# Attention of a hybrid block: values in two bursts, the query's norm in the exponential, and another spread of the filling work

## The chip, the cores and the metric

The kernel runs on one core of one Trainium2 chip. The metric is the device time of one launch in microseconds (us), as the median of several runs. A profile is one further execution, recorded by the hardware profiler; its rows give starts and durations of single instructions on the engines: PE (TensorE matmul) with PEld (its weight loads), DVE (VectorE), ACT (ScalarE), POOL (GpSimd) and SP (which here only issues DMAs).

## What is computed

The reference is a model of two layers over 512 latent tokens and 256 context tokens of width 1024: layer 0 mixes the tokens by attention, layer 1 by a state-space scan, and a gated feed-forward network follows each. The change touches only the attention, cut here to what matters:

```
q_l = rms_norm(q_l.reshape(bsz, seq, N_HEADS, HEAD_DIM), q_norm)    # 16 heads of 64
k_l = rms_norm(k_l.reshape(bsz, seq, N_KV_HEADS, HEAD_DIM), k_norm) # 4 key heads
q_l = apply_rope(q_l, cos, sin);  k_l = apply_rope(k_l, cos, sin)   # latent tokens only
s = jnp.einsum('bqhgd,bkhd->bhgqk', q, k) * (HEAD_DIM ** -0.5)
p = jax.nn.softmax(s, axis=-1)
o = jnp.einsum('bhgqk,bkhd->bqhgd', p, v)
x = x + mod_l[2] * (o.reshape(bsz, seq, Q_DIM) @ w_o)
```

Latent queries see all 768 keys; context queries see the 256 context keys. The norm of a query is one number per token and head: it multiplies the query's whole row of scores, so it can be applied before the scores are formed or after.

## The kernel before, in words

Activations lie transposed, with channels on the 128 partitions and tokens along the free axis. Products that need full precision are done by `mm3` (line 100): operands are split in a rounded high part and a low part in the type fp32r, and three matmuls add high·high, high·low and low·high. The attention's `score` (line 589) keeps both parts of a query stacked on the partitions, so two matmuls do. Transposes of probabilities (line 626) and the products with the values (line 638) are plain fp32; PE runs each value product as two passes.

**Units.** The 16 heads are handled in 8 pairs, p = 0 to 7. A pair has three units: `hf` 0 and 1 are 256 latent queries each against 768 keys, `hf` 2 the 256 context queries against 256 keys. Unit n = 3p + hf; there are 24. `a_steps` (line 597) makes a unit's scores and softmax: four score tiles of 128 queries by 768 keys, or four of 128 by 256 in two PSUM tiles. `softmax` (line 570) is a row maximum on DVE, the exponential with its sum on ACT, then a reciprocal and a scaling on DVE. `b_steps` (line 616) is the other half: for each of 6 (or 2) key tiles four transposes into one PSUM bank, a copy to SBUF (two of three on ACT, one on DVE, line 630), and, one step later, the product with the values for that key tile into the bank `ps_o`. The output is copied to `g.o[p]` (line 640).

**The loop** (lines 677 to 703) runs unit n's `a_steps` beside unit n-1's `b_steps`, a step of each in turn, and after every step `fill.run(us)`.

**Fill.** `Fill` (line 176) is a queue of generators with other work. `run(us)` takes pieces in order until their stated costs are over the budget `us`; a piece that returns `BREAK` costs 1.0 and rests for 5 calls. `require` runs a generator to its end at once. In the queue are the norm and rotation of keys and queries (`keys`, `queries`), the projection of the queries of pairs 4 to 7 (first half of `queries`, line 547), eight pieces `ada` (line 111, gains and biases from the conditioning: 2 MB of weights each), and, from pair 7 on, `project` (line 1221): the output projection w_o for pairs 0 to 2 and 3 to 4, through `down` (line 708), which adds the product to the residual `X` by one DVE instruction a tile (line 726). The last part of w_o, pairs 5 to 7, comes after the loop (line 1240). The budget is 0.65 us a step, 1.3 from unit 21 on.

**A query's preparation** (`normed`, line 512): square on ACT (`qsq`), gain on ACT, a swap of rows by four DMAs, three instructions of rotation (on POOL for most pairs), then `rstd_rows` (line 227): matmuls with a block of ones give sums over the 64 channels (`ssq`, line 236), some DVE and ACT instructions of 12 columns give the reciprocal root, one DVE instruction spreads it to 768 columns (`rbq`, line 247), six PE transposes turn it (`rsTq`, line 253), and two DVE instructions multiply the query (line 526). Then the casts to high and low parts (lines 564, 565).

**Order of the work.** In the first part of the attention (lines 392 to 489) the order is written out by hand. Behind it a planner orders the instructions of each engine: it takes them by program order as soon as, by its own model of durations, their inputs and tile slots are there; a later instruction can go ahead of one that has to wait. Each engine then executes that list strictly in order. What limits it are slots: 27 tiles `t3` of 768 columns, 6 tiles `t2` of 512, 10 tiles `t4` for weights, and in PSUM two tiles `S` for scores (two banks each) and four banks `B` for everything else.

Of the kernel before, what the change touches and what calls it, by code (L numbers as in the profile page):

```python
# [7 lines left out]
P = 128  # L8
# [102 lines left out]
def ada(g, src, layer, chunks, m0, nm, big=True):  # L111
# [17 lines left out]
    sb = g.t3p.tile([P, 512], F32, tag="t2", bufs=6, name="ada_sb")  # L129
# [41 lines left out]


# [54 lines left out]
def rstd_rows(g, sq, n, cols, width, name, bank):  # L227
# [16 lines left out]
    nc.vector.scalar_tensor_tensor(u, y, -0.5, u, ALU.mult, ALU.mult)  # L244
    rb = t3(g, f"rb{name}", n=n)
# [133 lines left out]
def attention(g, fill, X, late):  # L379
# [5 lines left out]
    t2 = lambda name, dt=F32: g.t3p.tile([P, 512], dt, tag="t2", bufs=6, name=name)  # L385
# [126 lines left out]
    def normed(qs, gain, eng):  # L512
# [9 lines left out]
        eng.tensor_tensor(qs[:, :L], qs[:, :L], sw, ALU.add)  # L522
        for r in rstd_rows(g, sq, T, g.blk, HD, "q", Bk):
            if r is not BREAK:
                pt, c0, c1 = r
                nc.vector.tensor_tensor(qs[:, c0:c1], qs[:, c0:c1], pt[:, : c1 - c0], ALU.mult)
            yield BREAK

    k2 = {}

    def keys(j, qs, eng):
        yield from normed(qs, kn, eng)
# [11 lines left out]
    qprep = {}  # L544

    def queries(p, qs, eng):
        if qs is None:
            w = load_w(g, I["wq"][p - 4], lo_engine="pool")
            qs = t3(g, "qs")
            for h, c0, n in ((hc, L, C), (hl, 0, L)):  # L550
                ps = Bk("ps_q")
                for k in range(KT):
                    ks = slice(k * P, (k + 1) * P)
                    mm3(g, (w[0][:, ks], w[1][:, ks]), [(ps[:, :n], h[k])], k == 0, k == KT - 1)
                    yield 3 * n / 2400
                nc.scalar.copy(qs[:, c0 : c0 + n], ps[:, :n])
            yield BREAK
        yield from normed(qs, g.qn8, eng)
# [11 lines left out]
    def softmax(pr, ps):  # L570
        mx = g.p.tile([P, 1], F32, tag="mx", bufs=4, name="mx")
        nc.vector.reduce_max(mx, ps, axis=AX.X, negate=True)
        sm = g.p.tile([P, 1], F32, tag="sm", bufs=4, name="sm")
        nc.scalar.activation(pr, ps, AF.Exp, bias=mx, accum_out=sm)
# [5 lines left out]
    class Unit:  # L580
# [16 lines left out]
        def a_steps(self):  # L597
            for e in range(2):
                if self.hf < 2:
                    for t in range(2):  # L600
# [3 lines left out]
                        softmax(pr, ps[:, :T])  # L604
                        self.pr[e, t] = pr
                        yield
                else:
                    ps, pr = Sb("ps_sc"), t2("prc")
                    for t in range(2):
# [3 lines left out]
                        softmax(self.pr[e, t], o)  # L613
                    yield

        def b_steps(self):

            nkt = self.nk // P
            po = None
            pts = []  # L620
            for kt in range(nkt + 1):
                if kt < nkt:
                    ps = Bk("ps_pt")
                    for e in range(2):
                        for t in range(2):
                            nc.tensor.transpose(ps[:, e * 256 + t * P : e * 256 + (t + 1) * P],  # L626
                                                self.pr[e, t][:, kt * P : (kt + 1) * P], g.ident)
                    pT = t2("pT")
                    copies[0] += 1
                    (nc.vector.tensor_copy if copies[0] % 3 == 0 else nc.scalar.copy)(pT, ps)  # L630
                    pts.append(pT)
                yield
                if kt:
                    if po is None:
                        po = Bk("ps_o")
                    v = vt[self.k0 // P + kt - 1][:, self.kv * HD : (self.kv + 1) * HD]
                    for e in range(2):
                        nc.tensor.matmul(po[S64[e], :256], v, pts[kt - 1][:, e * 256 : (e + 1) * 256],  # L638
                                         start=kt == 1, stop=kt == nkt)
# [733 lines left out]
```

## Time and profile before

| what | value |
|---|---|
| median of 3 runs (lowest, highest) | 1967.96 us (1965.83, 1969.62) |
| the profiled execution | 1956.99 us, its span 1955.2 us |
| PE, DVE, ACT, POOL busy in the span | 98%, 69%, 45%, 15% |
| attention loop and output projection in the trace (first score to last `ps_d` row before the tail) | 94.6 to about 443.4 us |
| of that, pairs 0 to 3 | 94.6 to 264.8 us |
| pairs 4 to 7, up to the last unit's first score | 264.8 to 391.5 us |
| the rest of the units and of w_o | 391.5 to 443.4 us |

How to read it: a row of the timeline has start, duration, engine, line, operation, output and inputs, shape and a count of merged instructions; a bracket at its end gives the idle time before it and what ended it. Matmuls are pipelined, so that the duration of one is longer than the time from its start to the start of the next; the time that PE spends on something is read from starts. Busy shares of PE are therefore no measure of how well it is used.

### The profile page before, as it was taken

Reading aid. Unit: us, or ns where it says so; the run is one execution under the profiler, and the core shown is the slowest. Engines: PE = TensorE matmul, PEld = TensorE weight load, DVE = VectorE, ACT = ScalarE, POOL = GpSimd, SP = SyncE. Lnnn points to the kernel's source line nnn. Section 1 sums busy time; section 2 is a strip of 40 time slices with the busy share of each in tenths; the row PEclk is TensorE's granted clock in tenths of the full one; section 3 lists DMA queues with packets and bytes.
Section 4 is the critical chain, followed back from the end, with each engine's and each line's share of the span. In section 5 each row is a group of like instructions: output and inputs, shape, how many; then the busy total and the mean of one; then the engine's idle time right before and its main releaser. Section 6 shows DMA issues by size and latency. Waiting matters only on the chain.

```text
span 1955.2 us, 28359 instructions
## 1 busy us (share of the span) xinstructions
PE 1909.6 (98%) x11068; PEld 1595.4 (82%) x11068; DVE 1346.6 (69%) x2119; ACT 885.1 (45%) x1636; POOL 297.5 (15%) x272
## 2 busy tenths in 40 slices
PE   8999999998999999999999999999999999999999
PEld 6866776688888888888888888888888888888887
DVE  4557778667877777775568777778878566555555
ACT  3645676436222222222256767666667343333331
POOL 2212201003000000000031233422335210000000
PEclk8999999999999999999999999999999999999999
DMA  8254010012434333332222433433354323333332
GB/s 330 87 183 162 28 33 17 1 55 98 143 125 123 128 124 123 123 106 65 76 87 66 134 119 108 121 116 92 103 162 119 101 74 96 97 97 97 97 98 87
DMA packets 71702, 205.36 MB, mean 105 GB/s; under 512 B 8720, under 2 KB 14224, under 8 KB 71440
## 3 DMA queue, kind: packets, MB, share of 16 engines
q1 hardware_dynamic: 71568, 203.54, 32.5%
q8 instruction: 87, 1.43, 0.3%
q14 instruction: 47, 0.39, 0.1%
HBM read 196.43 MB, written 4.46 MB: 103 GB/s over the span
## 4 chain that ended last, share of the span: by engine, by line
PE 70%; DVE 12%; issue 8%; POOL 4%; ACT 1%; DMA 1%; SPq 0%; POOLq 0%; DVEq 0%; ACTq 0%
PE ps_up L106 10%; PE ps_up L108 10%; PE ps_up L105 10%; PE ps_d L105 6%; PE ps_d L108 6%; PE ps_d L106 6%; PE ps_o L638 3%; PE ps_pt L626 3%; PE ps_s L594 2%; DVE xf L900 2%; POOL E L999 1%; DVE ht L281 1%; PE ps_in L108 1%; DVE E L1009 1%; DVE Bf L900 1%
## 5 line engine op out<-in xcount | busy, mean ns | idle before, releaser
L87 DVE TENSOR_TENSOR wl<-wst,wh 128x1024 fp32r<-128x1024 f32 x205 | 253.1, 1234 | 276.1 <-PE ps_up L106 124.1
L85 ACT CAST wh<-wst 128x1024 fp32r<-128x1024 f32 x211 | 221.1, 1049 | 413.3 <-DMA wst<-in_wup 323.7
L106 PE MATMUL ps_up<-hlf,wh 128*128 128x512 f32 x1008 | 357.0, 354 | 0.0
L105 PE MATMUL ps_up<-hhf,wh 128*128 128x512 f32 x1008 | 356.9, 354 | 0.0
L108 PE MATMUL ps_up<-hhf,wl 128*128 128x512 f32 x1008 | 356.8, 354 | 0.0
L106 PEld LDWEIGHTS ps_up<-hlf,wh 128*128 128x128 f32 x1008 | 190.6, 189 | 26.1
L105 PEld LDWEIGHTS ps_up<-hhf,wh 128*128 128x128 f32 x1008 | 190.5, 189 | 26.2
L108 PEld LDWEIGHTS ps_up<-hhf,wl 128*128 128x128 f32 x1008 | 190.5, 189 | 26.0
L105 PE MATMUL ps_in<-hhs,wh 128*128 128x512 f32 (+1 forms) x560 | 205.0, 366 | 0.0
L108 PE MATMUL ps_in<-hhs,wl 128*128 128x512 f32 (+1 forms) x560 | 199.7, 357 | 0.0
L106 PE MATMUL ps_in<-hls,wh 128*128 128x512 f32 (+1 forms) x560 | 199.5, 356 | 0.0
L105 PE MATMUL ps_d<-hdh,wh 128*128 128x512 f32 (+1 forms) x568 | 193.8, 343 | 1.4 <-DVE X L726 1.2
L108 PE MATMUL ps_d<-hdh,wl 128*128 128x512 f32 (+1 forms) x568 | 193.5, 341 | 0.0
L106 PE MATMUL ps_d<-hdl,wh 128*128 128x512 f32 (+1 forms) x568 | 193.0, 340 | 0.3 <-DVE hdl L87 0.3
L726 DVE SCALAR_TENSOR_TENSOR X<-ps_d,mod,X 128x512 f32<-128x512 f32 (+1 forms) x240 | 133.0, 584 | 31.3 <-PE ps_d L108 30.6
L106 PEld LDWEIGHTS ps_d<-hdl,wh 128*128 128x128 f32 x568 | 106.7, 188 | 15.5 <-DVE hdl L87 0.7
L105 PEld LDWEIGHTS ps_d<-hdh,wh 128*128 128x128 f32 x568 | 106.3, 188 | 15.3 <-DVE X L726 1.6
L105 PEld LDWEIGHTS ps_in<-hhs,wh 128*128 128x128 f32 x560 | 106.3, 190 | 15.1 <-issue 0.9
L108 PEld LDWEIGHTS ps_in<-hhs,wl 128*128 128x128 f32 x560 | 106.2, 190 | 14.9
L108 PEld LDWEIGHTS ps_d<-hdh,wl 128*128 128x128 f32 x568 | 106.7, 188 | 13.3
L106 PEld LDWEIGHTS ps_in<-hls,wh 128*128 128x128 f32 x560 | 106.3, 190 | 13.6
L167 DVE SCALAR_TENSOR_TENSOR junk<-wada,cb 128x1024 f32<-128x1024 f32 x96 | 116.7, 1215 | 1.1 <-ACT cb L159 0.9
(325 smaller groups left out, 3699.7 us busy)
## 6 DMA issues: line engine op xcount, KB each, us to landing
wst<-in_wup SPq DMA_DIRECT2D x88, 512.0 KB, 3.5
wada<-in_adaT SPq DMA_DIRECT2D x48, 512.0 KB, 3.5
wst<-in_win SPq DMA_DIRECT2D x48, 512.0 KB, 3.5
wst<-in_wdown SPq DMA_DIRECT2D x44, 512.0 KB, 4.1
wada<-in_adaB SPq DMA_DIRECT2D x32, 512.0 KB, 7.4
E<-ad SPq DMA_DIRECT2D x64, 256.0 KB, 6.5
ec<-ead SPq DMA_DIRECT2D x64, 128.0 KB, 4.3
wst<-in_wout SPq DMA_DIRECT2D x16, 512.0 KB, 3.5
```

The source lines that it names most:

```text
L85: keep(nc.scalar.copy(hi, src))
L87: keep(eng.tensor_tensor(lo, src, _r(hi), ALU.subtract))
L105: mm(out, wh, ah, start=first, stop=False)
L106: mm(out, wh, al, start=False, stop=False)
L108: mm(out, wl, ah, start=False, stop=last)
L167: g.tc.keep_in_program_order(nc.vector.scalar_tensor_tensor(junk, w, 1.0, cb[:, v * D : (v + 1) * D], ALU.mult, ALU.mult, accum_out=md[:, ...
L281: nc.vector.scalar_tensor_tensor(t[:, c0:c1], ap, g.moda[layer][ca][:, m, v : v + 1], rs[:, c0:c1], ALU.mult, ALU.mult)
L594: nc.tensor.matmul(ps[:, c0 : c0 + n], qprep[self.p][e][:, q0 : q0 + P], kk[:, self.k0 + c0 : self.k0 + c0 + n], start=i == 0, stop=i == 1)
L626: nc.tensor.transpose(ps[:, e * 256 + t * P : e * 256 + (t + 1) * P], self.pr[e, t][:, kt * P : (kt + 1) * P], g.ident)
L638: nc.tensor.matmul(po[S64[e], :256], v, pts[kt - 1][:, e * 256 : (e + 1) * 256], start=kt == 1, stop=kt == nkt)
L726: nc.vector.scalar_tensor_tensor(ap, o[:, c0:c1], gate[:, m, v : v + 1], ap, ALU.mult, ALU.add)
L900: nc.vector.scalar_tensor_tensor(cv, raw[:, tap : tap + n], par(f"sw{tap}", j), cv, ALU.mult, ALU.add)
```

## The change

The change does five things.

1. **Values in two bursts.** `b_steps` no longer multiplies with the values at every key tile. With six key tiles it multiplies three of them behind the fourth tile's transposes and three at the end; with two, both at the end. Within a burst the newest tile comes first.
2. **The norm in the exponential's scale.** `queries` ends its norm with the 12 columns of `rstd_cols` (the first part of the old `rstd_rows`) in a tile `qrs`; no spreading, no transposes, no multiplication of the query. `softmax` multiplies the negated maximum by the norm (a new DVE instruction of one column) and gives the norm to the exponential as `scale`. Keys are normed as before.
3. **Scores every second step.** `a_steps` yields twice after each score tile, so a unit takes 8 steps (before: 4, where both halves were short, else 8): 24 steps a pair instead of 20.
4. **Another queue.** The projections of pairs 4 to 7 are generators of their own, placed in the first half and required before unit 12; six of the eight `ada` are moved from the first half to the second. w_o for pairs 0 to 2 enters the queue at pair 4 and for pairs 3 to 4 at pair 6, and the outputs are split pair by pair.
5. **Budgets and slots.** `PACE` gives 0.5, 0.45, 0.35 us a step by `hf` in the first twelve units, 0.6, 0.5, 0.4 in the next twelve, and 1.0 at the end. `t2` has 8 slots instead of 6, `t3` 26 instead of 27.

```diff
+PACE = ((0.5, 0.45, 0.35), (0.6, 0.5, 0.4), (1.0, 1.0, 1.0))
...
-def rstd_rows(g, sq, n, cols, width, name, bank):
+def rstd_cols(g, sq, n, cols, width, name, bank):
...
     nc.vector.scalar_tensor_tensor(u, y, -0.5, u, ALU.mult, ALU.mult)
+    return u, y
+
+def rstd_rows(g, sq, n, cols, width, name, bank):
+    nc = g.nc
+    c = cols.shape[-1]
+    nt = n // P
+    u, y = rstd_cols(g, sq, n, cols, width, name, bank)
     rb = t3(g, f"rb{name}", n=n)
...
-    t2 = lambda name, dt=F32: g.t3p.tile([P, 512], dt, tag="t2", bufs=6, name=name)
+    t2 = lambda name, dt=F32: g.t3p.tile([P, 512], dt, tag="t2", bufs=8, name=name)
...
+    def projection(p):
+        w = load_w(g, I["wq"][p - 4], lo_engine="pool")
+        yield 0
+        qs = qraw[p] = t3(g, "qs")
...
+    def queries(p, eng):
+        qs = qraw[p]
+        sq = roped(qs, g.qn8, eng)
+        u, y = rstd_cols(g, sq, T, g.blk, HD, "q", Bk)
+        nc.vector.scalar_tensor_tensor(qrs[p], u, 1.5, y, ALU.add, ALU.mult)
+        yield BREAK
         out = []
...
-    def softmax(pr, ps):
+    def softmax(pr, ps, rs):
         mx = g.p.tile([P, 1], F32, tag="mx", bufs=4, name="mx")
         nc.vector.reduce_max(mx, ps, axis=AX.X, negate=True)
+        nc.vector.tensor_tensor(mx, mx, rs, ALU.mult)
         sm = g.p.tile([P, 1], F32, tag="sm", bufs=4, name="sm")
-        nc.scalar.activation(pr, ps, AF.Exp, bias=mx, accum_out=sm)
+        nc.scalar.activation(pr, ps, AF.Exp, bias=mx, scale=rs, accum_out=sm)
...
                         self.pr[e, t] = pr
                         yield
+                        yield
...
         def b_steps(self):
             nkt = self.nk // P
-            po = None
+            half = (nkt + 1) // 2
+            po = Bk("ps_o")
             pts = []
+            def multiply(k0, k1):
+                for kt in reversed(range(k0, k1)):
+                    v = vt[self.k0 // P + kt][:, self.kv * HD : (self.kv + 1) * HD]
+                    for e in range(2):
+                        nc.tensor.matmul(po[S64[e], :256], v, pts[kt][:, e * 256 : (e + 1) * 256],
+                                         start=kt == half - 1, stop=kt == half if nkt > half else kt == 0)
...
+                pts.append(pT)
+                if nkt > 2 and kt == half:
+                    multiply(0, half)
                 yield
...
+            yield
+            if nkt > 2:
+                multiply(half, nkt)
+            else:
+                half = nkt
+                multiply(0, nkt)
             nc.scalar.copy(g.o[self.p][:, self.q0 : self.q0 + 256], po[:, :256])
...
-    fill.q = [vals] + [kgen if o == "k" else adas.pop(0) if o == "a" else qgen[int(o)] for o in "a1aa2aa3aaa4k567"]
+    fill.q = [work[o]() for o in "aPa2Qk3RS4"]
...
             if A.p == 4:
                 fill.require(kgen)
-            if A.p == 7:
-                for p in range(6):
-                    osplit(p)
-                late()
+                for p in range(4, 8):
+                    fill.require(proj[p])
+                fill.q += [work[o]() for o in "5"]
+            if A.p >= 4:
+                while len(g.oT) < A.p - 1:
+                    osplit(len(g.oT))
+                late(A.p)
+                fill.q += [work[o]() for o in {4: "a", 5: "6", 6: "7aa", 7: "aaa"}[A.p]]
...
-            fill.run((.65, 1.3)[0] if n < 21 else (.65, 1.3)[1])
+            fill.run(PACE[n // 12][n % 3])
...
-    g.t3p, g.n3 = pool("pa", pha), 27
+    g.t3p, g.n3 = pool("pa", pha), 26
...
-    def late():
-        for fs in ((0, 1, 2), (3, 4), (5, 6, 7))[:-1]:
+    def late(p):
+        for fs in {4: ((0, 1, 2),), 6: ((3, 4),)}.get(p, ()):
             fill.add(project(fs))
```

In the queue's string a digit is a pair's `queries`, a letter P to S the projection of pairs 4 to 7, `k` the second keys and `a` the next `ada`.

More of the change, by code (lines that the diff above doesn't have):

```diff
@@ L659, in attention @@
             next(vals)
-    qgen = {p: queries(p, raw[{1: 2, 2: 4, 3: 5}[p]] if p < 4 else None, nc.gpsimd) for p in range(1, 8)}
+    qgen = {p: queries(p, nc.gpsimd) for p in range(1, 8)}
+    proj = {p: projection(p) for p in range(4, 8)}
     kgen = keys(1, raw[3], nc.gpsimd)
@@ L680, in attention @@
         if n == 1:
[L681 removed]
             for i, _ in enumerate(vals):
                 if i % 8 == 8 - 1:
[L684 to L685 removed]
+                    next(qgen[1], None)
         if A and A.hf == 0:
```

78 lines of the change are left out of this document (32 added, 46 removed).

## The prediction

> **What bounds the kernel now.** I read the page first, then busy times by stretch, then who waits for whom on PE, then PE's instructions in order of time.
>
> ```profile
> span 1955.2 us, 28359 instructions
> PE 1909.6 (98%) x11068; PEld 1595.4 (82%) x11068; DVE 1346.6 (69%) x2119; ACT 885.1 (45%) x1636; POOL 297.5 (15%) x272
> ```
> ```profile
> 94.60:443.41 348.81, 341.39 (x2234) 243.96 (x2235) 245.47 (x485) 191.07 (x403) 50.88 (x37) 0.99 0.20 67
> 264.80:391.50 126.70, 122.53 (x745) 84.93 (x744) 99.11 (x192) 77.25 (x166) 11.70 (x9) 1.00 0.05 13
> 324.30:354.10 29.80, 26.53 (x161) 16.21 (x160) 25.09 (x51) 18.34 (x40) 4.64 (x3) 1.00 0.03 7
> ```
> ```profile
> PE ps_s L594 <- ACT pr L574: 1.7, 3, 0.8
> ...
> PE ps_pt L626 <- DVE pr L576: 1.1, 2, 0.7
> ...
> PE rsTf L253 <- DVE rbf L247: 0.2, 1, 0.2
> ```
>
> The columns of a stretch are its length, then busy us of PE, PEld, DVE, ACT and POOL with instruction counts, clock, DMA share, GB/s. The attention and its output projection take 348.8 us, with PE busy for 341 of them and DVE for 245. The second fence is the list of PE's waits in that stretch: nine lines, from 1.7 down to 0.2 us, 8.1 us together. So PE is the bound there, almost without named waits; what the change can win must be PE time. The clock is full (0.99), so no gain comes from there.
>
> But busy does not mean that PE streams. The order of time shows it, around one value product between matmuls of w_o:
>
> ```profile
> 389.20 0.39 PE L106 MATMUL ps_d<-hlol,wh 128*128 128x512 f32 x1
> 389.43 0.40 PE L108 MATMUL ps_d<-hhol,wl 128*128 128x512 f32 x1
> 389.75 0.65 PE L638 MATMUL ps_o<-pT,v 128*64 128x256 f32 x4
> 390.33 0.39 PE L105 MATMUL ps_d<-hhoc,wh 128*128 128x256 f32 x1
> 390.56 0.28 PE L106 MATMUL ps_d<-hloc,wh 128*128 128x256 f32 x1
> 390.68 0.28 PE L108 MATMUL ps_d<-hhoc,wl 128*128 128x256 f32 x1
> ```
> ```profile
> 283.99 1.08 PE L638 MATMUL ps_o<-pT,v 128*64 128x256 f32 x8
> 285.00 0.38 PE L594 MATMUL ps_sc<-kh,q 128*128 128x256 f32 x1
> ...
> 285.35 0.60 PE L626 MATMUL ps_pt<-cst,pr 128*128 128x128 f32 x4
> 285.70 0.36 PE L105 MATMUL ps_q<-hha,wh 128*128 128x256 f32 x1
> 285.90 0.28 PE L106 MATMUL ps_q<-hla,wh 128*128 128x256 f32 x1
> ```
> ```profile
> 288.32 0.65 PE L638 MATMUL ps_o<-pT,v 128*64 128x256 f32 x4
> 288.90 0.66 PE L626 MATMUL ps_pt<-cst,pr 128*128 128x128 f32 x4
> 289.31 0.36 PE L105 MATMUL ps_q<-hha,wh 128*128 128x256 f32 x1
> 289.51 0.28 PE L106 MATMUL ps_q<-hla,wh 128*128 128x256 f32 x1
> ```
>
> From start to start a matmul of 512 columns takes 0.23 us in a row of its kind, one of 256 columns 0.12. The one before the value product takes 0.32: 0.09 more. The four passes of one key tile take 0.58 us, but eight take 1.01: the second four cost 0.43, so 0.15 of the 0.58 is paid once per group. The first matmul after it takes 0.23 where 0.12 is usual: 0.11. One **group** of value products costs 0.09 + 0.15 + 0.11 = 0.35 us beyond its work. In front of transposes it is somewhat less: the transposes behind it take 0.41 us (288.90 to 289.31) where they take 0.35 alone, so 0.09 + 0.15 + 0.06 = 0.30. I take 0.32.
>
> **The change part by part.**
>
> *Values in two bursts.* A unit with six key tiles has six groups now and two afterwards; one with two key tiles has two and then one. 16 × 6 + 8 × 2 = 112 groups become 16 × 2 + 8 = 40. The passes stay. 72 × 0.32 = **23.0 us less** on PE. The added waits: a burst needs the newest copy of `pT` first, and behind it on PE's list stand scores and fill; but the other tiles of a burst were copied a step or more earlier. One of the four `B` banks is now held from a unit's beginning; ACT and DVE empty the other banks in 0.6 to 0.7 us, so I charge nothing; if that cover failed, a transpose would wait for about one such copy.
>
> *The norm in the exponential.* On PE it takes away six transposes a query:
>
> ```profile
> L253 PE MATMUL rsTq<-cst,rbq x60: 270/272/332, 79.4 to 334.7; 128*128 128x128 f32 x60
> ```
>
> 60 less the keys' 12 are 48. Four cost 0.35 us alone and 0.41 behind values, 0.09 to 0.10 each: **4.2 us less** (about half, where they join a group of `ps_pt`; at most 4.9). On DVE:
>
> ```profile
> L247 DVE SCALAR_TENSOR_TENSOR rbq<-rsu,rsy 128x768 f32<-128x768 f32 x8 | 9.8, 1224 | 0.2
> L244 DVE SCALAR_TENSOR_TENSOR rsu<-rsy,rsu 128x12 f32<-128x12 f32 x8 | 4.7, 586 | 0.1
> L526 DVE TENSOR_TENSOR raw<-raw,rsTq 128x512 f32<-128x512 f32 x4 | 2.7, 685 | 5.8 <-issue 3.3 <-POOL raw L522 2.5
> L526 DVE TENSOR_TENSOR raw<-raw,rsTq 128x256 f32<-128x256 f32 x4 | 1.7, 413 | 3.0 <-PE rsTq L253 3.0
> ```
> ```profile
> L575 DVE RECIPROCAL sm<-sm x96: 143/155/167, 97.6 to 398.9; 128x1 f32<-128x1 f32 x96
> ```
> ```profile
> L243 DVE TENSOR_TENSOR rsu<-rsy,rsa x21: 149/171/1958, 13.1 to 1589.8; 128x12 f32<-128x12 f32 x10, 128x2 f32<-128x2 f32 x9, 128x4 f32<-128x4 f32 x2
> ```
>
> Eight queries lose about 8 × (1.22 + 0.69 + 0.41) = 18.6 us and get 8 × 0.59 = 4.7 for `qrs`. The 96 new one-column products are not in the trace; by the reciprocal of one column they cost 96 × 0.155 = 14.9 us, by the slowest small product seen 96 × 1.96 = 188, which only the worst instant allows; I take the reciprocal's price. DVE's sum stays about as it is (+1 us), and PE bears nothing. The page "GPSIMD Engine Reference" of the Trainium skill, section Specifications, speaks against this exchange: it says that VectorE contends with GpSimd where an instruction has two SBUF inputs, as the new product has and the reciprocal has not. The rows above agree, with 1958 ns at most against 167; by that rule, with POOL busy for 50.9 of 348.8 us, some 14 of the 96 would be held by up to 1.8 us, an estimate of at most 25 us of DVE time, which would enter the sum only where DVE is the bound.
>
> *Scores every second step, queue, budgets.* The work is the same; its places move. The four projections' weight loads with their POOL splits come earlier, six `ada` with 2 MB each and their DVE copies later, five w_o loads earlier than their place at pair 7. SP has room: the DMA share is 0.05 between 264.8 and 391.5. Pair 6 now has no fill: in the 29.8 us of the third stretch PE is idle for 3.3. With w_o there I take **3 us less**. The other way, the end loses its cover:
>
> ```profile
> 418.11 0.65 PE L638 MATMUL ps_o<-pT,v 128*64 128x256 f32 x4
> ...
> 418.81 0.37 ACT L640 COPY o<-ps_o 128x256 f32<-128x256 f32 x1 [1.65 <-PE ps_o L638]
> ...
> 421.06 0.41 DVE L87 TENSOR_TENSOR hloc<-o,hhoc 128x256 fp32r<-128x256 f32 x1
> ```
>
> The last values are copied and split while PE still does w_o for pairs 3 and 4; from 418.11 to the split's end at 421.47 are 3.4 us. Afterwards only w_o for pairs 5 to 7 is left, which needs this very output: I charge **3 us**. DVE stands at 99.1 of 126.7 us in the second half; with the PE time saved there (half of 27 us) that is 99.1 of 113, or 88%, in stretches without w_o. W_o itself dilutes it: its 120 pairs of products take 120 × (0.23 + 0.12) = 42 us of PE and these DVE instructions:
>
> ```profile
> L726 DVE SCALAR_TENSOR_TENSOR X<-ps_d,mod,X 128x256 f32<-128x256 f32 x29 | 13.9, 482 | 9.4 <-PE ps_d L108 9.3
> L726 DVE SCALAR_TENSOR_TENSOR X<-ps_d,mod,X 128x512 f32<-128x512 f32 x16 | 12.0, 749 | 12.4 <-PE ps_d L108 12.3
> ```
>
> 16 × (0.48 + 0.75) = 19.7 us, 47% of them. For queueing at a fuller DVE I charge **4 us**, an estimate between nothing and the 13.5 us of that half. One `t3` slot less and the four query tiles kept longer cost nothing as long as fill is ready.
>
> **Sum:** -23.0 - 4.2 - 3 + 3 + 4 = -23.2 us. The profiled execution (1956.99 us, 1.8 outside its span) would become 1933.8. The median of the runs shown, 11 us above it, becomes **1944.8 us** (-1.2%).
>
> **The rivals.**
>
> *DVE becomes the bound of the second half.* For it speaks 88%, against it the dilution. The half then keeps its length and its 13.5 us are lost, in place of my 4: -23.2 + 9.5 = -13.7, and with the same in the fuller stretches of the first half -8: 1954 to 1960 us.
>
> *The planner breaks the bursts.* It orders PE's list by its own model and may put ready instructions between. Against it: a burst begins with its newest tile, so all that follows is ready. If all 112 groups remained, only the transposes and the fill count: -4.2 - 3 + 3 + 4, about 0: 1968 us.
>
> *The transposes wait for the softmax (slower).* With six key tiles a unit's last score now comes two steps before the next unit's first transposes; before, it came one step ahead of them in a pair's first unit, but five in its second. The chain, in the stretch without fill:
>
> ```profile
> 338.42 0.50 PE L594 MATMUL ps_s<-kh,q 128*128 128x512 f32 x1 [0.77 <-ACT pr L574]
> 339.42 0.96 DVE L572 TENSOR_REDUCE mx<-ps_s 128x1 f32<-128x768 f32 x1
> 340.41 0.90 ACT L574 ACTIVATE pr<-ps_s,mx 128x768 f32<-128x768 f32 x1 [0.86 <-DVE mx L572]
> 342.41 0.61 DVE L576 TENSOR_SCALAR pr<-pr,sm 128x768 f32<-128x768 f32 x1
> 343.33 0.66 PE L626 MATMUL ps_pt<-cst,pr 128*128 128x128 f32 x4
> ```
>
> That is 4.9 us, and 5.1 with the new product; two steps of 24 a pair are 2 × 300 / 192 = 3.1 us (300 us: the stage afterwards without its tail). Without cover each of the 16 changes behind such a unit costs 2.0 us: +32 - 23 = +9, 1977 us. It decides from 1.45 us a change on. Against it speaks that a pair's first unit has a step less already, and that the waits of `ps_pt` on `pr` sum to 1.1 us in the whole stage.
>
> **How the numbers follow.** Chances: forecast 0.60 (1932 to 1954: waits gone at one end, DVE at the other), more (banks and waits all well) 0.06, DVE bound 0.14, bursts broken or gains cancelled 0.05, slower 0.15. A measurement can tell about 0.2%, 4 us, from no change. Faster 0.60 + 0.06 + 0.14 = 0.80, same 0.05, slower 0.15. The range leaves out the slower rival and the ends of the others: 1930 to 1963.
>
> **What would show it.** Stretches of twelve value passes in PE's order, about 40 in all, each some 0.15 us over 0.107 a pass; no `rsTq` beyond 12; the stretch from the first score to the last w_o product of about 326 us; PE's waits still near 8 us; DVE below 85% in the second half. I am wrong if waits on `pr`, `pT` or `ps_d` of tens of us appear, or if groups number far over 40.

## The result and the profile after

The changed kernel is **slower**: 1974.53 us median of 20 runs (1966.92 to 1981.88) against 1967.68 us (1959.40 to 1976.31) for the kernel before on the same chips, a ratio of 1.0032 with an interval of 1.0018 to 1.0046, or about 6.3 us. The forecast was 1944.8 us, and its range ended at 1963.

The profiled executions stand further apart, 1978.52 us against 1956.99: before's is faster than all its timed runs, after's lies near the upper end of its own. The clock that TensorE is granted differs between them as well: 0.994 and 0.984 as means of the two profiled spans, where the timed runs of the kernel before average 0.9897 (the 111 beside the experiments below) and the 20 of the changed kernel 0.9856. The traces therefore say where time went, and the timed ratios say how much.

The page of the changed kernel, its span, its busy row and its row of granted clock:

```profile
span 1976.7 us, 28337 instructions
...
PE 1903.2 (96%) x11020; PEld 1606.9 (81%) x11020; DVE 1347.1 (68%) x2199; ACT 891.5 (45%) x1636; POOL 298.4 (15%) x272
...
PEclk8998989989999999999999999999999999999999
```

The same row of the kernel before:

```profile
PEclk8999999999999999999999999999999999999999
```

PE is busy for 6 us less, and the span is longer all the same. The clock row has an 8 in slices 4, 6 and 9, all in the attention stage; before has 9 from the second slice on.

Busy times by stretch, from the first score to the first product of the feed-forward input, of the kernel before and then of the changed one (columns: stretch, length, then busy us of PE, PEld, DVE, ACT and POOL, clock, DMA share, GB/s):

```profile
94.00:449.43 355.43, 347.41 (x2286) 249.98 (x2286) 252.06 (x498) 195.91 (x414) 54.10 (x40) 0.99 0.20 66
```
```profile
94.00:465.76 371.76, 343.69 (x2258) 264.87 (x2258) 253.89 (x580) 205.61 (x418) 51.61 (x40) 0.94 0.19 64
```

PE idled for 355.43 - 347.41 = 8.0 us before and idles for 28.1 us now. And the clock is 0.94 where it was 0.99: over these lengths that is 0.06 × 371.76 = 22.3 us of lost clock against 3.6 (an upper bound, since the mean counts idle time too). Without that, PE's busy time is 343.8 us before and 321.4 now: 22.4 us less, where the forecast took away 23.0 + 4.2 = 27.2. So most of the gain is there, and two losses that the forecast did not have are larger: +20.1 us of idling and up to +18.7 of clock, in a stage that is 16.3 us longer.

The clock's part is that large in this pair of executions only. In the timed runs the mean clock falls from 0.9897 to 0.9856, about 8 us of a launch; with the work and the idling of the traces, -22.4 + 20.1 + 8 is +5.7 us, against the 6.3 measured.

The waits of PE in this stage of the changed kernel (us in all, times, longest):

```profile
PE ps_s L618 <- ACT pr L598: 6.6, 7, 2.4
PE ps_sc L618 <- ACT prc L598: 5.4, 6, 1.4
PE ps_s L618 <- DVE q L587: 4.7, 2, 2.8
PE ps_s L618 <- ACT prc L598: 2.5, 3, 1.4
...
PE ps_pt L662 <- DVE pr L600: 1.3, 2, 0.7
```

Three of these rows are a score that waits until an exponential gives back one of the two score tiles, 14.5 us together; one is a score that waits for a query. The waits of the transposes on the softmax, the place of the forecast's slower rival, are 1.3 us.

PE's order of time shows how a short wait becomes a slow stretch:

```profile
152.12 0.28 PE L618 MATMUL ps_s<-kl,q 128*128 128x256 f32 x1
...
154.00 0.50 PE L618 MATMUL ps_s<-kh,q 128*128 128x512 f32 x1 [1.60 <-ACT pr L598]
...
154.82 2.12 PE L239 MATMUL ssq<-cst,qsq 128*128 128x2 f32 x12
156.80 1.09 PE L662 MATMUL ps_pt<-cst,prc 128*128 128x128 f32 x4
157.69 1.71 PE L134 MATMUL ps_adt<-cst,ada_sb 128*128 128x2 f32 x8
...
162.72 0.58 PE L105 MATMUL ps_q<-hha,wh 128*128 128x256 f32 x1
163.10 0.42 PE L106 MATMUL ps_q<-hla,wh 128*128 128x256 f32 x1
163.31 0.41 PE L108 MATMUL ps_q<-hha,wl 128*128 128x256 f32 x1
...
165.76 0.28 PE L108 MATMUL ps_q<-hha,wl 128*128 128x256 f32 x1
165.87 0.28 PE L105 MATMUL ps_q<-hha,wh 128*128 128x256 f32 x1
```

PE waits 1.60 us for an exponential, then does twenty matmuls of two columns with four transposes between them. The four transposes at 156.80 take until 157.69, 0.89 us where the prediction saw 0.35. From 162.72 on, one matmul of 256 columns follows the other after 0.21 us; at 165.76 it is 0.11 again. The granted clock of this stretch agrees:

```profile
155.40:165.50 10.10, 10.10 (x45) 8.55 (x45) 6.09 (x14) 5.45 (x12) 3.79 (x3) 0.50 0.28 80
```

One wait of 1.6 us is followed by some ten us at half the rate.

### The profile page after: what moved, and what is told of

Its sections match the earlier page's. It is cut to its first block, busy times and chain, and to the rows that moved or that the text cites. A ratio compares the mean times of both kernels' runs of the same rounds, so it can differ in the third digit from the quotient of the medians.

```text
span 1976.7 us, 28337 instructions
## 1 busy us (share of the span) xinstructions
PE 1903.2 (96%) x11020; PEld 1606.9 (81%) x11020; DVE 1347.1 (68%) x2199; ACT 891.5 (45%) x1636; POOL 298.4 (15%) x272
## 4 chain that ended last, share of the span: by engine, by line
PE 70%; DVE 14%; issue 5%; ACT 3%; POOL 2%; DMA 1%; SPq 0%; POOLq 0%; ACTq 0%; DVEq 0%
PE ps_up L105 10%; PE ps_up L106 10%; PE ps_up L108 10%; PE ps_d L105 6%; PE ps_d L108 6%; PE ps_d L106 6%; PE ps_o L655 3%; DVE xf L940 2%; PE ps_in L108 2%; PE ps_in L105 2%; PE ps_in L106 2%; PE ps_s L618 2%; PE ps_pt L662 2%; DVE Bf L940 1%; DVE wl L87 1%
## 5 line engine op out<-in xcount | busy, mean ns | idle before, releaser
L105 PEld LDWEIGHTS ps_d<-hdh,wh 128*128 128x128 f32 x568 | 106.3, 188 | 15.3 <-DVE X L766 1.7
```

Source lines behind the costliest of these rows:

```text
L105: mm(out, wh, ah, start=first, stop=False)
```

## The experiments

Their ratios are to the kernel before, with a 95% interval; 0.1% is 2 us.

### Each part alone, on the kernel before

**bursts**: the new `b_steps`, with the slots of the change (`t2` 8, `t3` 26).

```diff
+            half = (nkt + 1) // 2
+            po = Bk("ps_o")
...
+                if nkt > 2 and kt == half:
+                    multiply(0, half)
```

> The kernel before with the values in two bursts alone (and the 8 and 26 slots that they need). Theory 'clock': rows of value passes and transposes without dense matmuls between them let PE's granted clock fall, so that the 23 us saved on group changes are spent at half clock: granted clock in the attention below 0.97 and a gain under 8 us. Rival 'order': the bursts are good by themselves and the new queue, steps and softmax chain bring the waits: about 45 value groups, PE's waits near 8 us, clock near 0.99, 15 to 23 us faster than before.

Measured: 0.9911 (0.9891 to 0.9932), 1951.23 us. **It beats both kernels.**

**slots**: the slots alone.

```diff
-    t2 = lambda name, dt=F32: g.t3p.tile([P, 512], dt, tag="t2", bufs=6, name=name)
+    t2 = lambda name, dt=F32: g.t3p.tile([P, 512], dt, tag="t2", bufs=8, name=name)
...
-    g.t3p, g.n3 = pool("pa", pha), 27
+    g.t3p, g.n3 = pool("pa", pha), 26
```

> The kernel before with the tile slots of the change alone (8 of 512 columns, 26 of 768). Theory: the bursts' gain of 0.9% is that of the bursts, so slots alone are within 3 us of before. Rival: the two more copies of transposed probabilities in flight, or the planner's other order, give part of it: 4 us or more faster.

Measured: 1.0028 (1.0011 to 1.0045), 1972.50 us. The mean clock of its runs is 0.9876, where the kernel before has 0.9896 beside it: some 4 of its 5.5 us. Against it the bursts are worth 0.9911 / 1.0028 = 0.9883, 23.0 us, or 18 to 28 by the two intervals. In the changed kernel's order of time, the bursts stand as the forecast wanted them:

```profile
416.87 1.52 PE L655 MATMUL ps_o<-pT,v 128*64 128x256 f32 x12
418.31 1.05 PE L134 MATMUL ps_adt<-cst,ada_sb 128*128 128x2 f32 x8
```

Twelve passes take 418.31 - 416.87 = 1.44 us, 12 × 0.107 + 0.15. In the whole order of time there are 41 groups of value products, 32 of them of twelve passes; the kernel before has 110.

**norm**: the query's norm in the exponential's scale, and nothing else.

```diff
+        nc.vector.tensor_tensor(mx, mx, rs, ALU.mult)
...
-        nc.scalar.activation(pr, ps, AF.Exp, bias=mx, accum_out=sm)
+        nc.scalar.activation(pr, ps, AF.Exp, bias=mx, scale=rs, accum_out=sm)
```

> The kernel before with the query's norm in the exponential's scale alone. Both theories see 48 transposes fewer (4 us of PE). Theory 'clock': nothing else changes, 2 to 5 us faster. Rival 'order': the exponential takes 0.99 instead of 0.91 us and waits for one more DVE product, so the chain from scores to transposes is about 0.3 us longer; PE's waits on ACT and DVE rise from 8 us to 15 or more and the kernel is no faster or up to 10 us slower.

Measured: 1.0078 (1.0053 to 1.0103), 1982.44 us, though 48 transposes and the multiplications of eight queries are gone. The largest of PE's waits, 1.7 us before, is now

```profile
PE ps_s L611 <- ACT pr L591: 10.2, 14, 1.3
```

**steps**: two yields a score tile, and the budget a step reduced in proportion.

```diff
                         yield
+                        yield
...
-            fill.run((.65, 1.3)[0] if n < 21 else (.65, 1.3)[1])
+            fill.run(.54 if n < 21 else 1.08)
```

> The kernel before with two steps a score tile alone, and the budget a step cut by 20/24 (0.54 and 1.08 us), so that the filling work spreads over a pair as before. Theory 'clock': within 4 us. Rival 'order': scores come later before the transposes that need them; PE's waits on ACT and DVE rise by 10 us or more, 5 to 15 us slower.

Measured: 1.0052 (1.0033 to 1.0071), 1976.85 us. Its largest waits on PE are value products on the copy of their probabilities, which the kernel before had for 0.7 us:

```profile
PE ps_o L640 <- DVE pT L632: 3.6, 2, 2.8
PE ps_o L640 <- ACT pT L632: 3.2, 5, 1.0
```

### What in the norm's move costs

**product**: the kernel before, with a product by one behind the maximum, as the changed kernel has one by the norm.

```diff
         nc.vector.reduce_max(mx, ps, axis=AX.X, negate=True)
+        nc.vector.tensor_tensor(mx, mx, g.ones[:, :1], ALU.mult)
```

> The kernel before with one more DVE product of one column (by ones) between the row maximum and the exponential; nothing is taken away. Theory 'chain': the two score tiles in PSUM are only given back when the exponential has read them, so 0.3 to 0.4 us more between maximum and exponential is waited for by the next score: 8 to 20 us slower, PE's waits of scores on the exponential up from 3.7 us to 10 or more. Rival 'planner': the chain has slack, and the norm variant was slow because its instructions were ordered otherwise: within 4 us of before.

Measured: 1.0079 (1.0059 to 1.0099), 1982.17 us: alone as much as the whole move of the norm.

**scale**: a column of ones as the exponential's scale.

```diff
-        nc.scalar.activation(pr, ps, AF.Exp, bias=mx, accum_out=sm)
+        nc.scalar.activation(pr, ps, AF.Exp, bias=mx, scale=g.ones[:, :1], accum_out=sm)
```

> The kernel before with the exponential's scale given as a column of ones instead of a constant; nothing else. The exponential should take 0.99 us instead of 0.91. Theory 'chain': 0.085 us more a score, a fifth of what the product adds with its hop: 2 to 5 us slower. Rival 'planner': no difference over 4 us.

Measured: 1.0012 (0.9996 to 1.0028), 1966.46 us; not told from nothing.

**product_off**: the same product, into a tile that nothing reads. DVE does all its work, but the exponential does not wait for it.

```diff
+        off = g.p.tile([P, 1], F32, tag="off", bufs=4, name="off")
+        nc.vector.tensor_tensor(off, mx, g.ones[:, :1], ALU.mult)
```

> The kernel before with the same 96 DVE products of one column by ones, into a column that nothing reads: beside the chain instead of in it. Theory 'chain length': the chain is as before, so within 5 us of before. Rival 'one more DVE instruction': DVE's 15 us and the planner's other order cost as much as in the chain, 10 us or more slower.

Measured: 0.9998 (0.9984 to 1.0013), 1967.45 us. **The same 96 instructions on the same engine cost nothing beside the chain and 0.79% in it.** It is not DVE's time.

**product_act**: the product in the chain, but on ACT.

```diff
+        nc.scalar.activation(mx, mx, AF.Identity, scale=g.ones[:, :1])
```

> The kernel before with one more instruction of one column (scaling by ones) between maximum and exponential, on ACT instead of DVE. Theory 'DVE list': the product was slow because reciprocals, scalings and copies stand between the maximum and it on DVE's strict list; on ACT it stands right before the exponential: under 6 us slower than before. Rival 'chain length': any instruction there costs about 16 us: 10 us or more slower.

Measured: 1.0053 (1.0033 to 1.0073), 1975.21 us. An instruction takes 0.295 us there, at the median, and 0.152 on DVE in product. DVE is freed of it and most of the cost stays; the intervals of this and of product overlap, so how much DVE's queue adds to the chain is not settled.

Whom the score tiles make wait, in product_off and then in product (us, times, of the idle time of the engine that uses the tile):

```profile
  DVE mx L572: 22.6, 29
...
  ACT pr L576: 6.5, 12
```
```profile
  DVE mx L573: 32.8, 30
...
  ACT pr L575: 11.8, 21
```

The second row of each is a score, or the load of its weights, that waits until the exponential has read the score tile: 12 times beside the chain, 21 in it. The first is the exponential waiting for its bias. In PE's own list of waits, scores wait on an exponential for 2.8 us in product_off, in 5 waits, and for 10.2 us in product, in 11, of which the largest rows are

```profile
PE ps_sc L595 <- ACT prc L575: 4.6, 4, 2.0
PE ps_s L595 <- ACT pr L575: 3.6, 5, 1.2
```

And the stretch from the first score to the first product of the feed-forward input, of product_off, of product and of norm:

```profile
94.00:454.07 360.07, 351.97 (x2300) 254.78 (x2298) 263.24 (x596) 196.68 (x416) 51.52 (x40) 0.98 0.19 65
94.00:466.98 372.98, 357.80 (x2286) 256.83 (x2286) 265.83 (x594) 195.55 (x414) 52.71 (x40) 0.97 0.18 63
94.00:471.80 377.80, 358.36 (x2247) 251.01 (x2248) 253.22 (x580) 206.29 (x419) 51.09 (x40) 0.98 0.18 62
```

The profiled execution of product_off lies in the middle of its runs, as those of product and norm do, so it is the one to compare with. In product PE idles for 15.2 us, 7.1 more, about what the waits on exponentials grew by, and the clock takes up to 4.0 us more (0.03 × 372.98 against 0.02 × 360.07): 11.1 of the 12.9 us by which the stretch is longer. In norm PE idles for 11.3 us more at the same clock, and is busy for 6.4 us more although its transposes are fewer; where that comes from is open. The timed runs agree on the clock: 0.9873 for product against 0.9897 beside it, 4.8 us of 15.5, and 0.9893 for norm against 0.9895, nothing of 15.3. So the loss is in the main waiting, not clock. How much of it is the planner's other order, which moves the time in slots too, is not separated; in product_off, with as many instructions, another order cost nothing.

The same reading goes for the changed kernel. These are the exponentials on ACT before, then in the changed kernel (busy us, mean ns, idle time before and what ended it):

```profile
L574 ACT ACTIVATE pr<-ps_s,mx 128x768 f32<-128x768 f32 x64 | 57.9, 905 | 22.4 <-DVE mx L572 22.2
...
L574 ACT ACTIVATE prc<-ps_sc,mx 128x256 f32<-128x256 f32 x32 | 15.1, 474 | 10.9 <-DVE mx L572 10.6 <-DVE sm L575 0.2
```
```profile
L598 ACT ACTIVATE pr<-ps_s,mx,qrs 128x768 f32<-128x768 f32 x64 | 63.4, 991 | 68.7 <-DVE mx L596 66.9 <-PE ps_sc L618 1.7
...
L598 ACT ACTIVATE prc<-ps_sc,mx,qrs 128x256 f32<-128x256 f32 x32 | 17.9, 562 | 15.3 <-DVE mx L596 15.0
```

ACT now stands still for 81.9 us before its exponentials until DVE has the bias, where it was 32.8: half a microsecond more for each of 96. Each exponential is 0.09 us longer as well.

### What lowers the clock

**gate** computes nothing of the reference and writes zeros: PE does series of one kind of work each, with dense matmuls between the series.

```diff
+    trans(440)
...
+    pv(112)
...
+    adal(56)
...
+    narrow(120)
...
+    latency(14, 4)
...
+    latency(9, 10)
```

> Computes nothing of the reference and writes zeros: rows of one kind of PE work, each about 24 us, with 90 dense fp32r matmuls of 512 columns between them: transposes; value passes (64 columns of weights, 256 moved); conditioning passes (32 columns of weights); matmuls of 2 columns; the mixture of transposes, value passes and 2-column matmuls of the last units; the same mixture with dense matmuls between; and dense matmuls in groups of 4 and of 10 with a DVE copy of the result to wait for in between. Theory 'clock': the granted clock falls to about 0.5 in at least one of the rows in which PE never waits (2-column matmuls or the mixture), and not in dense rows. Rival: it falls only where PE waits, in the groups of 4, and stays at 1.0 in every row without waits.

Measured in one execution, by stretches inside the series, in the columns used above: transposes, value passes, `ada` passes, matmuls of two columns, a mixture like that of the last units, groups of 4 dense matmuls that each wait for a DVE copy of the one before, groups of 10 that do.

```profile
30.00:75.00 45.00, 45.00 (x411) 44.86 (x410) 0.00 (x0) 0.00 (x0) 0.00 (x0) 1.00 0.00 1
100.00:122.00 22.00, 22.00 (x208) 14.64 (x206) 0.00 (x0) 0.00 (x0) 0.00 (x0) 1.00 0.00 1
145.00:155.00 10.00, 10.00 (x100) 2.99 (x92) 0.00 (x0) 0.00 (x0) 0.00 (x0) 1.00 0.01 2
190.00:220.00 30.00, 30.00 (x143) 30.00 (x142) 0.00 (x0) 0.00 (x0) 0.00 (x0) 0.50 0.01 1
246.00:271.00 25.00, 25.00 (x212) 18.53 (x207) 0.00 (x0) 0.00 (x0) 0.00 (x0) 1.00 0.01 1
360.00:390.00 30.00, 21.38 (x42) 11.95 (x42) 7.61 (x11) 0.00 (x0) 0.00 (x0) 0.50 0.00 0
413.00:430.00 17.00, 13.08 (x53) 9.14 (x52) 3.46 (x5) 0.00 (x0) 0.00 (x0) 1.00 0.00 0
```

The clock is 1.00 or 0.50 in these stretches, nothing between, and 1.00 too in the eighth series, the mixture with dense matmuls between. It halves in two of eight: with matmuls of two columns back to back, without any wait, and in groups of 4 with a wait behind each. Transposes, value passes and the mixture keep it full. These are the two things that stand in the slow stretch above, `ssq` and `ps_adt` rows and a short wait. That each slow stretch of the changed kernel has just these causes is argued from this, not shown. Of its six slow stretches in the attention stage, five begin behind 3.4 us in which PE idled for 0.5 to 2.4 us. Ahead of the sixth and longest PE does not idle:

```profile
418.20:421.60 3.40, 3.40 (x30) 3.17 (x29) 1.12 (x6) 2.00 (x5) 0.00 (x0) 1.00 1.02 395
421.60:435.20 13.60, 12.25 (x58) 7.65 (x57) 6.12 (x20) 5.02 (x11) 0.00 (x0) 0.50 0.11 43
```

In the first of these rows 2.0 us of PE go to sixteen matmuls of two columns (`ps_adt`); the mixture in gate, at 1.00, has eight of them in 3.36 us.

### The changed kernel with one part put back

**after_nonorm**: the old norm of the queries and the old softmax.

```diff
-        nc.vector.tensor_tensor(mx, mx, rs, ALU.mult)
...
-        nc.scalar.activation(pr, ps, AF.Exp, bias=mx, scale=rs, accum_out=sm)
+        nc.scalar.activation(pr, ps, AF.Exp, bias=mx, accum_out=sm)
```

> The changed kernel with the old norm of the queries (spread, transposed and multiplied before the casts) and the old softmax. Theory 'chain': the norm's move is what costs: 8 to 18 us faster than the changed kernel, so 0.3% to 0.6% faster than before, PE's waits on the exponential under 8 us. Rival 'order': steps and queue make the waits, and with 48 transposes more it is as slow as the changed kernel or slower (0.3% to 0.6% slower than before).

Measured: 1.0060 (1.0043 to 1.0077), 1978.46 us: not faster than the changed kernel's 1.0032, though the move of the norm alone costs 0.78%.

**after_nosteps**: one yield a score tile.

```diff
-PACE = ((0.5, 0.45, 0.35), (0.6, 0.5, 0.4), (1.0, 1.0, 1.0))
+PACE = ((0.52,) * 3, (0.6,) * 3, (1.0,) * 3)
...
-                        yield
```

> The changed kernel with one step a score tile as before, and budgets of 0.52, 0.6 and 1.0 us a step so that a pair keeps its filling work. Theory 'chain': scores come earlier before their transposes, but the chain is as long: 3 to 10 us faster than the changed kernel, about as fast as before. Rival 'order': the late scores are the main loss: 10 us or more faster than the changed kernel, faster than before by 0.2% or more.

Measured: 1.0101 (1.0082 to 1.0120), 1985.74 us. Again the opposite of the part alone. Its waits say where:

```profile
PE ps_s L618 <- ACT pr L598: 14.7, 13, 3.3
PE ps_s L618 <- DVE q L587: 7.6, 2, 5.8
```

With the longer chain, scores that follow each other faster wait longer for a score tile, and queries are later.

**after_oldqueue**: the queue of before, projections inside `queries`, w_o at pair 7.

```diff
-    fill.q = [work[o]() for o in "aPa2Qk3RS4"]
+    fill.q = [vals] + [kgen if o == "k" else adas.pop(0) if o == "a" else qgen[int(o)] for o in "a1aa2aa3aaa4k567"]
...
-            fill.run(PACE[n // 12][n % 3])
+            fill.run(.54 if n < 21 else 1.08)
```

> The changed kernel with the queue of before (projections inside the queries, ada early, w_o from pair 7 on) and budgets of 0.54 and 1.08 us a step; bursts, norm and steps as changed. Theory 'queue': late and forced query preparation, ada in the second half and w_o between the units bring the waits and with them the halved clock: 8 us or more faster than the changed kernel, so faster than before. Rival 'chain': the product between maximum and exponential and the late scores do; the queue is neutral: within 5 us of the changed kernel.

Measured: 1.0033 (1.0016 to 1.0050), 1975.55 us. With the old queue the parts simply add: -0.89 + 0.78 + 0.52 = +0.41%, measured +0.33. The new queue as a whole, from 1.0033 to 1.0032, is worth nothing.

**after_qearly**: the changed kernel with its queries earlier: pair 4's ahead of the projection of pair 7, those of pairs 6 and 7 first in the queue.

```diff
-    fill.q = [work[o]() for o in "aPa2Qk3RS4"]
+    fill.q = [work[o]() for o in "aPa2Qk3R4S"]
...
-                fill.q += [work[o]() for o in {4: "a", 5: "6", 6: "7aa", 7: "aaa"}[A.p]]
+                fill.q = [work[o]() for o in {5: "6", 6: "7"}.get(A.p, "")] + fill.q
+                fill.q += [work[o]() for o in {4: "a", 6: "aa", 7: "aaa"}.get(A.p, "")]
```

> The changed kernel with the queries of pairs 4, 6 and 7 placed earlier in the queue, so that none is prepared only when its first unit begins. Theory 'queue': PE's waits of scores on the query's split (4.7 us, and the stretch at 264 to 276 us in which the clock then halves) go: 5 to 12 us faster than the changed kernel. Rival 'chain': within 3 us of it, the waits reappear on the exponential.

Measured: 0.9991 (0.9972 to 1.0010), 1965.68 us, 0.41% better than the change. The row of scores that wait for a query is gone from its list of waits. So the late queries cost some 8 us, and the mean clock of the timed runs, 0.9888 against 0.9856, makes about 6 of them. As the new queue as a whole is worth nothing, something else in it should give as much back; that is inferred, and no run shows it.

**after_adaearly**: all `ada` in the first half again, the budgets 0.125 us a step higher there and lower in the second half, everything else of the queue as changed. If `ada` near the end had lowered the clock, this would have been faster.

```diff
-    fill.q = [work[o]() for o in "aPa2Qk3RS4"]
+    fill.q = [work[o]() for o in "aaPaa2aaQaak3RS4"]
```

> The changed kernel with seven of the eight ada in the first half as before, and budgets 0.125 us a step higher there and lower in the second half. Theory 'clock': the stretch at 420 to 436 us, with three ada and their 2-column matmuls among the last units, no longer runs at half clock: 4 to 8 us faster than the changed kernel. Rival: the last units are then without cover and wait for the softmax: within 3 us or slower.

Measured: 1.0095 (1.0074 to 1.0117), 1986.04 us. That theory held in its place and failed in the sum. From 400 us on, the changed kernel and then this one, and this one's whole stage:

```profile
400.00:465.76 65.76, 62.76 (x446) 45.78 (x444) 41.87 (x100) 31.08 (x67) 10.02 (x12) 0.90 0.42 152
400.00:475.03 75.03, 67.34 (x480) 56.08 (x480) 52.26 (x123) 39.21 (x88) 13.90 (x15) 0.98 0.06 19
94.00:475.03 381.03, 345.32 (x2260) 267.30 (x2258) 254.55 (x582) 207.48 (x420) 52.02 (x40) 0.93 0.18 62
```

The end has its clock back, but from 94 to 260 us, where the `ada` stand now, the clock is 0.88, against 0.94 in the changed kernel; the kernel before has its `ada` there too, at 0.98, so it is not `ada` alone. PE idles for 35.7 us, 7.6 more. The rival, that the end lacks cover, can account for a part at most: from 380 us on PE idles for 8.4 us, and for 5.1 in the changed kernel.

### Which parts go together

Four runs kept the bursts and left other parts out, or moved the product.

**bursts_queue** is after_nonorm with one yield and the budgets of after_nosteps: bursts with the new queue.

```diff
-PACE = ((0.5, 0.45, 0.35), (0.6, 0.5, 0.4), (1.0, 1.0, 1.0))
+PACE = ((0.52,) * 3, (0.6,) * 3, (1.0,) * 3)
```

> The bursts with the changed queue and budgets (0.52, 0.6 and 1.0 us a step), without the norm's move and with one step a score tile. Theory 'queue': the queue alone undoes the bursts' gain of 16 us: between 0.2% faster and 0.8% slower than before, PE's waits over 18 us. Rival 'chain': without the product the gain stays: 0.5% or more faster than before.

Measured: 1.0070 (1.0045 to 1.0095), 1983.53 us, against 0.9911 with the old queue: here the new queue and its budgets cost 1.6%. Its waits name the old norm, whose spreading and transposes a query that is late already still has to go through:

```profile
PE rsTq L266 <- DVE rbq L260: 6.1, 3, 3.0
PE ps_s L617 <- DVE q L588: 4.6, 2, 2.5
```

**bursts_qearly** is the same with the queue of after_qearly.

```diff
-    fill.q = [work[o]() for o in "aPa2Qk3RS4"]
+    fill.q = [work[o]() for o in "aPa2Qk3R4S"]
```

> The bursts with the changed queue, the queries earlier, one step a score tile and the old norm. If late queries were what the queue cost: 0.6% or more faster than before, as fast as the bursts alone. If ada and w_o among the units cost as well: slower than the bursts alone by 8 us or more.

Measured: 1.0041 (1.0023 to 1.0059), 1971.71 us. Late queries are a part of it, but 1.3% between this and bursts remain.

**qearly_nonorm** is after_nonorm with that queue.

```diff
-    fill.q = [work[o]() for o in "aPa2Qk3RS4"]
+    fill.q = [work[o]() for o in "aPa2Qk3R4S"]
```

> The changed kernel with the queries placed earlier and the old norm of the queries and softmax. Both theories: no product at all, but 48 transposes (4 us) and a longer preparation of the queries, which can be late again. If the product is what holds the gain back: 0.4% to 0.9% faster than before. If the queue is: no faster than the changed kernel.

Measured: 1.0069 (1.0043 to 1.0094), 1979.82 us.

**qearly_act** is after_qearly with the product on ACT.

```diff
-        nc.vector.tensor_tensor(mx, mx, rs, ALU.mult)
+        nc.scalar.activation(mx, mx, AF.Identity, scale=rs)
```

> The changed kernel with the queries placed earlier and the product on ACT. Theory 'DVE list': 6 to 14 us faster than with the product on DVE, 0.3% to 0.8% faster than before. Rival 'chain length': within 4 us of the variant with early queries, so about as fast as before.

Measured: 1.0005 (0.9983 to 1.0027), 1965.00 us; not told from after_qearly.

So of all versions the bursts alone are the fastest, and the best of the complete change, with its queries early, only comes back to the time before.

## Why the prediction was wrong, step by step

**Values in two bursts: right.** Forecast -23.0 us, measured -23.0 against the slots alone (-17.5 with them), and 69 groups are gone where 72 were forecast. That the two figures are the same is luck: the measured one is known to 5 us, and some 4 us of it are clock, 0.9876 for slots and 0.9897 for bursts. The added waits, put at nothing, are there: in the trace of bursts scores wait 9.1 us for exponentials, 2.6 before.

**The norm in the exponential: this step failed.** The forecast gave 4.2 us to PE, put the 96 products down as time of DVE's, "and PE bears nothing". Measured for the move alone is +15.3 us, some 20 us off, and the product alone has the same cost; PE bears it, since 10.2 us of its waits in product are scores that wait for an exponential. The product's price was right: its row in the changed kernel is

```profile
L596 DVE TENSOR_TENSOR mx<-mx,qrs x96: 140/156/1920, 99.4 to 426.9; 128x1 f32<-128x1 f32 x96
```

156 ns at the median, 0.155 forecast, and 1920 at most, as the forecast's sentence on GpSimd allowed. Wrong was where it stands: between the maximum and the exponential, in the chain that ends with one of only two score tiles coming free. The prediction had that chain in hand, "4.9 us, and 5.1 with the new product", and used it only for the transposes. Its other use, score, maximum, product, exponential, next score, has little reserve: a later score has to wait until one of the two tiles is free. That 96 × 0.16 us come to 15 us is no proof that each product stood in the way: PE waited for an exponential 11 times in product, not 96, and up to 4 us are clock.

**Scores every second step, queue, budgets: failed at two places.** "The work is the same", and 0 us: the steps alone cost 0.52%, 10 us, and the slots, "cost nothing as long as fill is ready", 0.28%, 5.5 us. The first has waits of value products on their copies beside it. For the slots no wait stands out, and some 4 us are clock; they let the planner order the whole stage anew, and what in that order costs is open. The missing fill of pair 6 (-3) and the lost cover at the end (+3) can't be told apart: the new queue as a whole came to nothing, as their sum did, but with 8 us of late queries in it that the forecast did not have. The four projections stand ahead of the query of pair 4 in the queue, and w_o ahead of those of pairs 6 and 7; the prediction listed what moves and did not ask what it is moved in front of.

**DVE at 88%: no bound.** product_off adds all the products to DVE and costs nothing (-0.02%). In the changed kernel DVE is busy for 111.0 of the 151.2 us from 264.8 to 416.0 us, 73%. The 4 us charged for queueing have nothing to show for them.

**"The clock is full, so no gain comes from there."** True, and the prediction did not turn the sentence round: a full clock can be lost. About 8 us of the changed kernel's timed runs are that, and up to 18.7 us in the pair of traces.

**The slower rival** came near in value, 1977 against 1974.5, and failed in its place: transposes wait 1.3 us for the softmax, and scores wait for the exponential. Its chain was the right one, followed to one user out of two. The waits of PE, which were to stay near 8 us, come to 28.7 us.

The sum by measured parts with the old queue is -17.5 + 15.3 + 10.2 = +8.0 us, with +6.5 measured for after_oldqueue. What stays open: why the new queue costs 1.3% beside bursts alone, even with early queries; `ada` later and w_o earlier were not tried one by one there.

## What to carry to other kernels

An instruction has a price and a place: before giving it the price of its engine's spare time, follow each chain that it joins to the resource that the chain gives back, and count how many of those there are; the same product of 0.15 us, 96 times, cost 15.5 us in such a chain and nothing beside it. When work is moved in a queue, look at what it now stands in front of, and by when that is needed. Parts of a change can each be measured alone and still not add up with a new order of the work, so measure the best part by itself: here it was the whole gain.

## What the hardware showed that was not expected

The clock that TensorE is granted halves on short waits. In the gate run, groups of 4 dense matmuls with a DVE copy between them run at 0.50, groups of 10 at 1.00; one such group, in its order of time:

```profile
363.93 2.08 PE L1233 MATMUL ps_mm<-R,loop 128*128 128x512 f32 x4 [0.78 <-DVE loop L1234]
366.79 2.08 PE L1233 MATMUL ps_mm<-R,loop 128*128 128x512 f32 x4 [0.78 <-DVE loop L1234]
```

The wait is 0.78 us in a period of 2.86, or of 1.98 in the first groups, still at full clock. The Trainium skill's page "TensorE: Matmul & The Clock Gate", section "HAM oscillation — how this bites in real kernels", gives as its abstract rule "no PE-idle gaps >~3.4µs"; here a gap of a quarter of that is enough when the groups are short, which the measurement decides. The section after it, "A second HAM failure mode: psum-queue depth-cycling", has a kernel whose clock oscillates with short idle times between groups of matmuls; the run agrees that such idle times lower it, and here it stayed at 0.50 until the groups ended. The same page's Part 4 says of transposes that the full clock "doesn't engage" for them; the series of 440 float32 transposes here, matmuls with an identity in the rows, has 1.00.

Matmuls of two columns, 143 in 30 us without any idle time, halve the clock by themselves. An exponential of 128 × 768 from PSUM takes 991 ns with a column as its scale and 905 with a constant; the run scale, with that alone, took no time that could be told from nothing.
